# First three modulation sums on TensorE in four column groups, squares ahead of the scaling, three ScalarE products per later sum, and an output projection that is 512 columns wide

## The chip, the cores and the metric

The kernel runs on one core of one Trainium2 chip. The metric is the device time of one execution in microseconds (us). The profile is of one execution; its engines are PE (TensorE matmuls), PEld (TensorE weight loads), DVE (VectorE), ACT (ScalarE), POOL (GpSimd) and SP (the queue that issues most DMAs). "L185" is line 185 of the kernel's file; the changed kernel's lines have other numbers below the first edit.

## The reference

One transformer block on 512 tokens of width 1024, in fp32. What matters here:

```python
c_act = jax.nn.silu(c)
mod = jnp.dot(c_act, ada_w[l]) + ada_b[l]
sh1, sc1, g1, sh2, sc2, g2 = jnp.split(mod, N_MOD, axis=-1)
h = modulate(rms_norm(x, norm1_g[l]), sh1, sc1)          # h*(1+scale)+shift
z = jnp.einsum('bsd,de->bse', h, w_in[l]) + b_in[l]      # q, k, v, gates of two branches
...                                                       # mLSTM branch, attention branch
x = x + g1[:, None, :] * jnp.einsum('bsd,de->bse', merged, w_out[l])
h = modulate(rms_norm(x, norm2_g[l]), sh2, sc2)
...                                                       # gated FFN, then a last rms_norm
```

## The kernel before, in words

All matmuls with weights run as three passes of fp32r (`mm3`, L197 to L201): high part by high part, high by low, low by high. Weights come from HBM in chunks; `cvt` makes the high part (a cast on ACT, L183) and the low part (a subtraction on DVE, L185). Each engine works its own queue in the order in which the code is written; the order is set by hand, and for later stages by a planner that counts the time of each matmul (`spend`).

**The first stage (L475 to L577).** The rows of x (four tiles of 128 tokens, two halves each) are squared, normalised and scaled (`normed`, L408), two tiles at a time: sums of squares of tiles 0 and 1, their reciprocal root, their scaling, then the same for tiles 2 and 3. TensorE turns the tiles (`turn_x`), ACT keeps the turned tiles (`keep_x`). The stage then computes seven blocks of 128 output columns over eight blocks k of the width: 21 matmuls of 512 columns per k (`g1_mm`, L554, order in L567 to L577: seven with the high weights, seven with the low weights, seven with the low part of h). Each k needs its own tile of h (`h_tile`, L512: high part `hh` on ACT, low part `hl` on DVE), and that needs the modulation of block k: shift and scale, a sum over eight products of a 128x256 piece of `ada_w` with a column of silu(c), and over the 128 partitions.

For k = 0 TensorE does this whole sum with 16 fp32 matmuls (L500). For k = 1 to 7 `ada_fast` (L271) shares the products out: POOL multiplies and adds two (three for k = 1), DVE multiplies and adds four (three), ACT multiplies two, POOL adds all, and `ada_cols` (L304) sums over the partitions with two one-column matmuls against ones. `ada_put` (L298) writes shift and scale with two small DVE instructions. In each k from 2 on, at the ninth matmul, `ahead` (L532) sends out: the cast of the next weights, the sum for k+2, the modulation and h tile of k+1, the low part of the next weights.

POOL also works out the angles of the rotary embedding: half of them ahead of the stage (`next(turns)`, L477), half behind the last modulation sum (L575). ACT takes their sine and cosine (L565, L566) ahead of the results of the stage, which it moves out of PSUM (`padded`, L589). The convolutions, the gates (L849) and all later work follow from there; L754 is where TensorE turns the gates.

**The output projection (L1206 to L1324).** `project` multiplies a tile of 128 tokens of the merged branches (eight blocks of the width, stationary) by a chunk of `w_out`. A chunk holds all eight row blocks of 256 output columns, so there are four chunks, 16 calls, each with 24 matmuls of 256 columns. Each result is multiplied by the gate and added to x on DVE (L1227, L1229, 256 wide); `squares` sums the squares on ACT, `normed2` finishes the second norm for two token tiles, and `h2_part` turns and modulates the result for the FFN. The FFN begins with token tiles 0 and 1 (`first`, L1340) while tiles 2 and 3 are being finished.

Of the kernel before, what the change touches and what calls it, by code (L numbers as in the profile page):

```python
# [40 lines left out]
def _chunks():  # L41
# [18 lines left out]
    for q in range(4):  # L60
        got.append(("w_out", 0, 8, 256 * q, 256))
# [38 lines left out]
def block_kernel(ctx, tc, x, wall, adaw, pcol, prow, positions, inv_freq, out):  # L100
# [60 lines left out]
    def cvt(n, half, what=None, eng=None):  # L161
# [19 lines left out]
        s = slice(0, SIZES[n]) if half is None else slice(half * h, half * h + h)  # L181
        if what != "lo":
            A.copy(hi[:, s], raws[n][:, s])  # L183
# [87 lines left out]
    def ada_fast(j, pools, vs, scaled, between=None):  # L271
        p = small([128, 256], "accp", 3)
        for k in pools:
            t = small([128, 256], "prod", 2) if k else p
            G.tensor_scalar(t[:], araw[j][k], cact[:, k:k + 1], 1.0, op0=ALU.mult, op1=ALU.mult)
            if k:
                G.tensor_tensor(out=p[:], in0=p[:], in1=t[:], op=ALU.add)
        a = small([128, 256], "accv", 2)
        for k in vs:
            if k == vs[0]:  # L280
                V.tensor_scalar(a[:], araw[j][k], cact[:, k:k + 1], None, op0=ALU.mult)
            else:
                V.scalar_tensor_tensor(out=a[:], in0=araw[j][k], scalar=cact[:, k:k + 1], in1=a[:],
                                       op0=ALU.mult, op1=ALU.add)
            if between and k == vs[1]:
                between()
        for t in (scaled() if callable(scaled) else scaled) + [a[:]]:
            G.tensor_tensor(out=p[:], in0=p[:], in1=t, op=ALU.add)  # L288
        return p
# [14 lines left out]
    def ada_cols(b, j, acc):  # L304
        pb = bank("c")
        for q in range(2):
            PE.matmul(pb[:, q:q + 1], acc[:, blk(q)], ones[:, 0:1], start=True, stop=True)
# [45 lines left out]
    A.activation(cact[:], cols[:, 0:8], AF.Silu)  # L353
    hcol = const.tile([128, 60], F32, name="hcol")
# [44 lines left out]
    def rms_tiles(tiles):  # L399
        n = len(tiles)  # L400
        ss = small([128, 5, n], f"ss{n}", 3)
# [3 lines left out]
        rms_finish(ss, D)  # L405
        return [ss[:, 3, i:i + 1] for i in range(n)]

    def normed(tiles, between=None):  # L408
        rs = rms_tiles(tiles)
        if between:  # L410
            between()
        got = [[T(), T()] for _ in tiles]
        for q in range(2):
            for i, r in enumerate(rs):
                if i % 2 == q:
                    V.tensor_scalar(got[i][q][:], tiles[i][q][:], r, None, op0=ALU.mult)
                else:
                    A.activation(got[i][q][:], tiles[i][q][:], AF.Copy, scale=r)
        return got
# [57 lines left out]
    next(turns)  # L477

    wb = bank("c")
# [4 lines left out]
    xb = [bank(t) for t in ("m", "m", "a", "a", "a")]  # L484
    ab = [bank("b"), bank("c")]
# [5 lines left out]
    def keep_x(k):  # L491
        xnT[k] = T()
        A.copy(xnT[k][:], xb[k][:])

    for k in range(5):
        turn_x(k, (0, 1))
    xn += normed(xt[2:4])
    for k in range(KD):
        for q in range(2):
            PE.matmul(ab[q][:, :128], araw[0][k][:, blk(q)], cact[:, k:k + 1].to_broadcast([128, 128]),  # L500
                      start=k == 0, stop=k == KD - 1)
    for k in range(5):
        turn_x(k, (2, 3))
    ada_put(0, 0, ab[0][:, 0:1], ab[1][:, 0:1])
    xb += [bank(t) for t in "bbc"]
    for k in range(5, KD):
        turn_x(k, range(NT))
# [4 lines left out]
    def h_tile(k):  # L512
        src = xnT[k] if k else xb[0]
# [3 lines left out]
        V.tensor_scalar(hf[:], src[:], modA[:, k:k + 1], modB[:, k:k + 1], op0=ALU.mult, op1=ALU.add)  # L517
        V.tensor_tensor(out=pr[1][:], in0=hf[:], in1=pr[0][:].bitcast(F32), op=ALU.subtract)
        hT.append(pr)

    cvt(0, None)
    h_tile(0)
    for k in range(1, 5):
        keep_x(k)
    accs = ada_fast(1, range(3), (5, 6, 7), ada_scaled(1, (3, 4)))
    cvt(1, None)
    for k in (5, 7, 6):
        keep_x(k)
    g1 = [bank(t) for t in ("m", "m", "a", "a", "a", "b", "b")]
    for k in range(KD):  # L530
        wh, wl = parts[k]
        def ahead():  # L532
# [5 lines left out]
            def following():  # L538
                ada_cols(0, k + 1, ready)
                h_tile(k + 1)  # L540

            if k + 2 < KD:
                accs = ada_fast(k + 2, (0, 1), (2, 3, 4, 5),
                                (lambda: ada_scaled(2, (6, 7))) if k == 0 else ada_scaled(k + 2, (6, 7)),
                                None if k else following)
                if k + 4 < KD:
                    ada_fetch(k + 4)
            if 0 < k < KD - 1:
# [23 lines left out]
        for n, (m, e) in enumerate(order):  # L572
            if n == (16, 14, 8)[min(k, 2)]:
# [635 lines left out]
    def parts_of(n):  # L1209
        return tuple(t.rearrange("p (k n) -> p k n", k=8) for t in parts[n])  # L1210

    nb = [0]

    def project(ch, ci, tiles, n=0):
        pbs = []
        for _ in tiles:
            pbs.append(bank(mb[nb[0] % 4]))
            nb[0] += 1
# [318 lines left out]
```

## Time and profile before

| | us |
|---|---|
| three timed runs | 800.43, 801.29, 801.38 (median 801.29) |
| the profiled execution | 800.23, of which the span from first to last instruction is 798.4 |
| mean granted TensorE clock | 0.996 |

| engine | busy us | share of the span |
|---|---|---|
| PE | 781.0 | 98% |
| PEld | 652.7 | 82% |
| DVE | 410.1 | 51% |
| POOL | 323.5 | 41% |
| ACT | 306.8 | 38% |

The shares are means over stages that differ. From 30 to 50 us DVE and POOL are busy for more than 90% of the time, elsewhere mostly for less than 70%. A matmul's row shows when it started and a modelled end that overlaps the next one's start, so the pace of matmuls is read from the distance of their starts. A row's part in brackets is the idle time of the engine ahead of it and what ended it.

### The profile page before, as it was taken

What the parts mean: (1) busy time and instruction counts of PE and PEld (TensorE: products, weight loads), DVE (VectorE), ACT (ScalarE), POOL (GpSimd) and SP (SyncE); (2) the same over time, 40 slices, a digit from 0 to 9 for tenths busy, and PEclk for the clock granted to TensorE, in tenths of its full rate; (3) what the DMA queues carried; (4) which work ended last, traced back from release to release, by engine and by line L of the source; (5) the groups of instructions that cost most, each with busy time, mean ns of one, the idle gap of its engine ahead of it and who ended that gap; (6) DMA issues with size and microseconds to landing.
All of it is one profiled execution on the core that took longest, in us unless ns stands there. A gap on an engine that the chain in (4) does not pass through costs nothing.

```text
span 798.4 us, 10508 instructions
## 1 busy us (share of the span) xinstructions
PE 781.0 (98%) x4049; PEld 652.7 (82%) x4049; DVE 410.1 (51%) x665; ACT 306.8 (38%) x535; POOL 323.5 (41%) x446
## 2 busy tenths in 40 slices
PE   8899999999999999999999999999999999999995
PEld 8678988778877787788999988888888888888884
DVE  6986778665575553477557333222322324333257
ACT  6538654324454444323257322212222213333234
POOL 7894436899965878950002695000000000000013
PEclk9999999999999999999999999999999999999998
DMA  8936224345421432345222325532233232222002
GB/s 316 377 118 225 106 80 151 100 172 211 159 106 54 155 109 106 140 186 202 75 86 106 118 107 173 234 107 67 93 105 106 106 105 106 99 67 99 1 0 106
DMA packets 23538, 102.52 MB, mean 128 GB/s; under 512 B 3512, under 2 KB 3648, under 8 KB 13888
## 3 DMA queue, kind: packets, MB, share of 16 engines
q1 hardware_dynamic: 21664, 99.74, 34.8%
q10 hardware_dynamic: 1824, 2.12, 1.0%
q8 instruction: 32, 0.52, 0.3%
q14 instruction: 18, 0.15, 0.1%
HBM read 97.65 MB, written 2.10 MB: 125 GB/s over the span
## 4 chain that ended last, share of the span: by engine, by line
PE 83%; DVE 7%; POOL 4%; ACT 3%; issue 1%; DMA 1%; SPq 0%; POOLq 0%; DVEq 0%; ACTq 0%
PE psm L198 14%; PE psm L200 14%; PE psm L199 14%; PE psb L198 9%; PE psb L200 9%; PE psb L199 9%; PE psa L200 2%; PE psa L198 2%; PE psa L199 2%; POOL accp L288 2%; PE psa L1038 1%; PE psc L1096 1%; DVE x L1433 1%; PE psb L1079 1%; DVE t L611 1%
## 5 line engine op out<-in xcount | busy, mean ns | idle before, releaser
L185 DVE TENSOR_TENSOR whl<-raw,whl 128x1024 fp32r<-128x1024 f32 (+1 forms) x124 | 159.0, 1292 | 181.4 <-ACT whl L183 181.3
L183 ACT CAST whl<-raw 128x1024 fp32r<-128x1024 f32 (+1 forms) x124 | 127.7, 1050 | 277.3 <-PE psb L200 162.2
L1436 POOL TENSOR_TENSOR t<-x,v 128x512 f32<-128x512 f32 x6 | 7.8, 1306 | 284.1 <-DVE x L1433 279.6
L251 POOL TENSOR_TENSOR accp<-accp,prod 128x256 f32<-128x256 f32 x112 | 89.9, 803 | 9.3
L198 PE MATMUL psb<-t,whl 128*128 128x512 f32 (+1 forms) x224 | 84.4, 377 | 0.0
L198 PE MATMUL psm<-t,whl 128*128 128x512 f32 (+1 forms) x224 | 84.3, 376 | 0.0
L200 PE MATMUL psb<-t,whl 128*128 128x512 f32 (+1 forms) x224 | 84.0, 375 | 0.0
L200 PE MATMUL psm<-t,whl 128*128 128x512 f32 (+1 forms) x224 | 83.8, 374 | 0.0
L199 PE MATMUL psm<-t,whl 128*128 128x512 f32 (+1 forms) x224 | 83.8, 374 | 0.0
L199 PE MATMUL psb<-t,whl 128*128 128x512 f32 (+1 forms) x224 | 83.8, 374 | 0.0
L198 PE MATMUL psm<-hh,whl 128*128 128x512 f32 x192 | 77.4, 403 | 0.5 <-ACT x L1020 0.5
L248 POOL TENSOR_SCALAR prod<-ada,cact 128x256 f32<-128x256 f32 x112 | 75.6, 675 | 0.0
L200 PE MATMUL psm<-hh,whl 128*128 128x512 f32 x192 | 75.0, 391 | 0.0
L199 PE MATMUL psm<-hl,whl 128*128 128x512 f32 x192 | 74.9, 390 | 0.0
L200 PEld LDWEIGHTS psb<-t,whl 128*128 128x128 f32 x224 | 42.1, 188 | 7.9 <-DVE whl L185 0.2
L200 PEld LDWEIGHTS psm<-t,whl 128*128 128x128 f32 x224 | 42.2, 188 | 7.5
L199 PEld LDWEIGHTS psm<-t,whl 128*128 128x128 f32 x224 | 42.2, 188 | 7.5
L199 PEld LDWEIGHTS psb<-t,whl 128*128 128x128 f32 x224 | 42.2, 188 | 7.5
L198 PEld LDWEIGHTS psm<-t,whl 128*128 128x128 f32 x224 | 42.2, 188 | 7.4
L198 PEld LDWEIGHTS psb<-t,whl 128*128 128x128 f32 x224 | 42.2, 188 | 7.3
L198 PEld LDWEIGHTS psm<-hh,whl 128*128 128x128 f32 x192 | 36.1, 188 | 8.1 <-ACT x L1020 0.7
L200 PEld LDWEIGHTS psm<-hh,whl 128*128 128x128 f32 x192 | 36.0, 188 | 8.2 <-DVE whl L185 0.4
(371 smaller groups left out, 1635.9 us busy)
## 6 DMA issues: line engine op xcount, KB each, us to landing
raw<-in_dram SPq DMA_DIRECT2D x59, 1024.0 KB, 4.8
ada<-in_dram SPq DMA_DIRECT2D x16, 1024.0 KB, 4.8
t<-in_dram SPq DMA_DIRECT2D x30, 256.0 KB, 5.8
x<-in_dram SPq DMA_DIRECT2D x16, 256.0 KB, 5.7
raw<-in_dram SPq DMA_DIRECT2D x8, 448.0 KB, 6.1
v<-in_dram SPq DMA_DIRECT2D x8, 256.0 KB, 5.6
t<-t ACTq DMA_DIRECT2D x32, 64.0 KB, 2.1
out_dram<-t SPq DMA_DIRECT2D x8, 256.0 KB, 2.1
```

The source lines that it names most:

```text
L183: A.copy(hi[:, s], raws[n][:, s])
L185: (eng or V).tensor_tensor(out=lo[:, s], in0=raws[n][:, s], in1=hi[:, s].bitcast(F32), op=ALU.subtract)
L198: PE.matmul(o, lh, rh, start=start, stop=False)
L199: PE.matmul(o, lh, rl, start=False, stop=False)
L200: PE.matmul(o, ll, rh, start=False, stop=stop)
L248: G.tensor_scalar(t[:], rv[:, k, :], cact[:, k:k + 1], 1.0, op0=ALU.mult, op1=ALU.mult)
L251: G.tensor_tensor(out=p[:], in0=p[:], in1=t[:], op=ALU.add)
L288: G.tensor_tensor(out=p[:], in0=p[:], in1=t, op=ALU.add)
L611: V.scalar_tensor_tensor(out=y[:, e:], in0=zr[:, :512 - e], scalar=hcol[:, 32 - e * 8 + m:33 - e * 8 + m], in1=y[:, e:], op0=ALU.mult, op1 ...
L1038: PE.matmul(bs[e][:, o:o + n], qp[a][r, blk(i)], kp[b][r, :n], start=g == 0, stop=g == 2)
L1079: PE.transpose(tb[:, o + (i - j) * 128:o + (i - j + 1) * 128], es[i][:, blk(j)], ident[:])
L1096: PE.matmul(yb[e * 64:e * 64 + 64, 128 * j:512], av[j][:, (2 * p + e) * 64:(2 * p + e + 1) * 64], t[j], start=j == 0, stop=j == NT - 1)
```

## The change

Five things are changed together.

1. The modulation sums of k = 0, 1 and 2 are computed on TensorE. The stationary operand is 32 equal columns of silu(c), the moving operand the 128x256 piece of `ada_w`; products k and k+4 go to output partitions 32(k mod 4) and up, four column groups in one PSUM bank. ACT copies the bank out, and two one-column matmuls with a column that is 1 on one partition of each group add the four groups and turn the result. For k = 1 they are sent out behind the sixth matmul of k = 0, for k = 2 behind the fourth of k = 1.
2. For k = 3 to 7 ACT does three products rather than two, the first of which is the start of DVE's sum; DVE's own first product goes.
3. The sums of squares of all four x tiles are started ahead of the first scaling, POOL does three of the eight scalings, all four tiles are turned for six of eight k (the other two inside k = 0), the first 640 columns of the first weights are cast by POOL, and the first half of the angles stands behind that cast on POOL.
4. The code that emits the work ahead is placed at other matmuls for k = 0 and 1.
5. A chunk of `w_out` holds four row blocks of 512 columns. `project` then does 12 matmuls of 512 columns per call, the second chunk adds to the first one's bank, and gating, adding to x and squaring are 512 wide.

```diff
-        got.append(("w_out", 0, 8, 256 * q, 256))
+        got.append(("w_out", 512 * (q % 2), 4, 512 * (q // 2), 512))
...
+    def ada_rows(j):
+        pb = bank("c")
+        for k in range(8):
+            g = slice(k % 4 * 32, k % 4 * 32 + 32)
+            PE.matmul(pb[g, :256], cact32[:, k, :], araw[j][k], start=k < 4, stop=k >= 4)
+        t = T()
+        A.copy(t[:, 0:256], pb[:, 0:256])
+        return t
+
+    def ada_fast(j, pools, vs, scaled):
...
+        lead, *rest_ = ada_scaled(j, scaled)
         a = small([128, 256], "accv", 2)
         for k in vs:
-            if k == vs[0]:
-                V.tensor_scalar(a[:], araw[j][k], cact[:, k:k + 1], None, op0=ALU.mult)
...
+            V.scalar_tensor_tensor(out=a[:], in0=araw[j][k], scalar=cact[:, k:k + 1],
+                                   in1=lead if k == vs[0] else a[:], op0=ALU.mult, op1=ALU.add)
+        for t in rest_ + [a[:]]:
             G.tensor_tensor(out=p[:], in0=p[:], in1=t, op=ALU.add)
...
-    for _ in range(23):
+    for _ in range(30):
         PE.matmul(wb[:, :128], ident[:], ones, start=True, stop=True)
-    xn = normed(xt[0:2])
+    xn = [[T(), T()] for _ in range(NT)]
+    s01 = sums(xt[0:2])
+    rms_open(s01, D)
+    s23 = sums(xt[2:4])
+    rms_close(s01)
+    for i, q, eng in ((0, 0, V), (1, 0, A), (0, 1, G), (1, 1, G)):
+        scaled_by(eng, xn[i][q], xt[i][q], s01[:, 3, i:i + 1])
+    rms_open(s23, D)
+    rms_close(s23)
+    for i, q, eng in ((2, 0, V), (3, 0, A), (2, 1, V), (3, 1, G)):
+        scaled_by(eng, xn[i][q], xt[i][q], s23[:, 3, i - 2:i - 1])
...
+    for k in range(6):
         turn_x(k, (0, 1))
+    r0 = ada_rows(0)
+    for k in range(2):
         turn_x(k, (2, 3))
+    keep_x(0, V)
+    ada_cols(0, 0, r0, sel4[:], "b")
+    for k in range(2, 6):
+        turn_x(k, (2, 3))
...
+    cvt(0, slice(0, 640), "hi", G)
+    next(turns)
+    keep_x(1)
+    h_tile(0, lambda: cvt(0, slice(0, 640), "lo"))
...
-                accs = ada_fast(k + 2, (0, 1), (2, 3, 4, 5),
...
+            if 1 < k < KD - 2:
+                accs = ada_fast(k + 2, (0, 1), (2, 3, 4), (5, 6, 7))
...
-            if n == (16, 14, 8)[min(k, 2)]:
+            if k == 0 and n == 4:
+                for kk in (7, 6):
+                    turn_x(kk, range(NT))
+                for kk in (7, 5, 6):
+                    keep_x(kk)
+            if n == (6, 4, -1)[min(k, 2)]:
+                third = early()
+            if n == (13, 10, 8)[min(k, 2)]:
                 ahead()
...
+    def project(ch, half, i, q):
+        if half == 0:
+            pbank[i] = bank(mb[i])
+        pb = pbank[i]
+        for k in range(4):
+            m = mg[4 * half + k]
+            mm3(pb[:], m[0][:, blk(i)], m[1][:, blk(i)], ch[0][:, k, :], ch[1][:, k, :],
+                half == 0 and k == 0, half == 1 and k == 3)
+        if half:
+            tm = T()
+            V.tensor_tensor(out=tm[:], in0=pb[:], in1=g1row[q][:], op=ALU.mult)
...
     def squares(i, q):
-        h = xr[i][0][:] if q == 0 else xr[i][1][:, (q - 1) * 256:q * 256]
         junk = T()
-        A.activation(junk[:, :512 if q == 0 else 256], h, AF.Square, accum_out=sq[:, q, i:i + 1])
+        A.activation(junk[:], xr[i][q][:], AF.Square, accum_out=ss2[i // 2][:, q, i % 2:i % 2 + 1])
```

On DVE, around the first reciprocal root of the first stage (`ss` holds the sums, `x` are halves of x tiles), before the change:

```order
L392 SCALAR_TENSOR_TENSOR ss_36_240<-ss_36_240 128x1 x2
L393 SCALAR_TENSOR_TENSOR ss_36_240<-ss_36_240 128x2
L416 TENSOR_SCALAR t_256<-x_87,ss_36_240 128x512
L416 TENSOR_SCALAR t_259<-x_92,ss_36_240 128x512
L376 SCALAR_TENSOR_TENSOR t_282,ss_52_281<-x_95 128x512
L376 SCALAR_TENSOR_TENSOR t_286,ss_52_281<-x_99 128x512
```

and now:

```order
L388 SCALAR_TENSOR_TENSOR t_260,ss_48_259<-x_95 128x512
L388 SCALAR_TENSOR_TENSOR t_264,ss_48_259<-x_99 128x512
L401 RECIPROCAL ss_43_247<-ss_43_247 128x2
L404 SCALAR_TENSOR_TENSOR ss_43_247<-ss_43_247 128x1 x2
L405 SCALAR_TENSOR_TENSOR ss_43_247<-ss_43_247 128x2
L424 TENSOR_SCALAR t_239<-x_87,ss_43_247 128x512
```

The squares of tiles 2 and 3 (`x_95`, `x_99`) stood behind the scaling of tiles 0 and 1 and now stand ahead of their reciprocal.

On TensorE inside k = 0 of the first stage there is nothing but matmuls with weights (`whl`) in the kernel before. Now this stands there (`cact` is silu(c), `t_113` to `t_119` the modulation weights of k = 1, `sel` the selecting column):

```order
L578 MATMUL psm_372<-hh_358,whl_337 128x512
L276 MATMUL psc_399<-t_113,cact_169 32x256 x2
L276 MATMUL psc_399<-t_115,cact_169 32x256 x2
L276 MATMUL psc_399<-t_117,cact_169 32x256 x2
L276 MATMUL psc_399<-t_119,cact_169 32x256 x2
L578 MATMUL psm_373<-hh_358,whl_337 128x512
L578 MATMUL psa_374<-hh_358,whl_337 128x512
L578 MATMUL psa_375<-hh_358,whl_337 128x512
L578 MATMUL psa_376<-hh_358,whl_337 128x512
L578 MATMUL psm_372<-hl_359,whl_337 128x512
L578 MATMUL psm_373<-hl_359,whl_337 128x512
L578 MATMUL psa_374<-hl_359,whl_337 128x512
```

Eight matmuls of 256 columns in four groups came in between.

On DVE in a later k (here k = 4; `accv` is DVE's part of the sum for k+2), before:

```order
L281 TENSOR_SCALAR accv_602<-t_494,cact 128x256
L283 SCALAR_TENSOR_TENSOR accv_602<-t_494,cact,accv_602 128x256
L283 SCALAR_TENSOR_TENSOR accv_602<-t_496,cact,accv_602 128x256 x2
L300 SCALAR_TENSOR_TENSOR modA<-psc_618,adb_170,cols 128x1
L302 TENSOR_TENSOR modB<-psc_618,cols 128x1
L517 TENSOR_SCALAR t_623<-t_363,modA,modB 128x512
L518 TENSOR_TENSOR hl_625<-t_623,hh_624 128x512
L185 TENSOR_TENSOR whl_591<-raw_452,whl_591 128x896
```

and now:

```order
L291 SCALAR_TENSOR_TENSOR accv_607<-t_492,cact,t_601 128x256
L291 SCALAR_TENSOR_TENSOR accv_607<-t_492,cact,accv_607 128x256
L291 SCALAR_TENSOR_TENSOR accv_607<-t_494,cact,accv_607 128x256
L306 SCALAR_TENSOR_TENSOR modA<-psc_622,adb_178,cols 128x1
L308 TENSOR_TENSOR modB<-psc_622,cols 128x1
L527 TENSOR_SCALAR t_627<-t_368,modA,modB 128x512
L530 TENSOR_TENSOR hl_629<-t_627,hh_628 128x512
```

One instruction of eight went; the first that is left reads ACT's product `t_601`.

## Rows read from the trace of the kernel before

**Rows 1.** Waits of PEld over the whole run: total us, times, longest.
```profile
PEld psm L556 <- DVE whl L185: 3.6, 5, 1.0
PEld psa L754 <- DVE gates L849: 0.9, 1, 0.9
```

**Rows 2.** Chain of waits, followed back from 110 or 100 us: start, us, what.
```profile
55.17 0.80 POOL accp L288
...
62.24 0.37 ACT t L565
...
91.68 0.27 PE psa L754
```

**Rows 3.** Timeline of DVE in k = 4: start, us, engine, line, what.
```profile
45.84 0.48 DVE L281 TENSOR_SCALAR accv<-t,cact 128x256 f32<-128x256 f32 x1
...
46.36 2.33 DVE L283 SCALAR_TENSOR_TENSOR accv<-t,cact,accv 128x256 f32<-128x256 f32 x3
...
50.64 1.08 DVE L185 TENSOR_TENSOR whl<-raw,whl 128x896 fp32r<-128x896 f32 x1
...
51.64 0.48 DVE L281 TENSOR_SCALAR accv<-t,cact 128x256 f32<-128x256 f32 x1
```

**Rows 4.** Timeline of PE in the first stage.
```profile
17.76 0.48 PE L556 MATMUL psm<-hh,whl 128*128 128x512 f32 x1
...
18.62 0.50 PE L556 MATMUL psm<-hh,whl 128*128 128x512 f32 x1 [0.38 <-DVE t L517]
...
31.19 0.73 PE L556 MATMUL psm<-hh,whl 128*128 128x512 f32 x2 [0.30 <-ACT hh L516]
...
40.42 0.50 PE L307 MATMUL psc<-ones_r,accp 128*128 128x1 f32 x4
...
40.78 0.47 PE L556 MATMUL psm<-hh,whl 128*128 128x512 f32 x1
```

**Rows 5.** Timeline ahead of the first stage, all engines.
```profile
5.39 0.69 DVE L376 SCALAR_TENSOR_TENSOR t<-x 128x512 f32<-128x512 f32 x1
...
8.98 0.17 DVE L389 RECIPROCAL ss<-ss 128x2 f32<-128x2 f32 x1 [0.23 <-ACT ss L384]
...
10.05 1.21 DVE L416 TENSOR_SCALAR t<-x,ss 128x512 f32<-128x512 f32 x2
...
11.87 0.39 PE L500 MATMUL psb<-cact,v 128*128 128x128 f32 x2
...
15.44 0.60 PE L489 MATMUL psm<-ident,t 128*128 128x128 f32 x4
```

**Rows 6.** Timeline of SP: the DMA that is issued when a slot is free.
```profile
9.84 0.33 SPq L260 DMA_DIRECT2D t<-in_dram  x1
```

**Rows 7.** Groups by line and shape: busy us, mean ns of one, idle before.
```profile
L1021 POOL TENSOR_SCALAR t<-t 128x512 f32<-128x512 f32 x8 | 4.9, 618 | 0.6 <-ACT t L1020 0.6
...
L1190 DVE TENSOR_TENSOR t<-t,psb 128x512 f32<-128x512 f32 x4 | 2.7, 679 | 0.0
```

**Rows 8.** Timeline of PE: fp32 matmuls in two column groups, and what follows.
```profile
251.89 2.38 PE L1096 MATMUL psc<-t,t 128*64 128x512 f32 x16
...
254.19 0.50 PE L198 MATMUL psm<-hh,whl 128*128 128x512 f32 x1
```

**Rows 9.** Timeline of PE: 24 matmuls of 512 columns, and the whole projection.
```profile
66.22 0.39 PE L198 MATMUL psc<-hh,whl 128*128 128x512 f32 x1
...
71.43 0.39 PE L200 MATMUL psc<-hh,whl 128*128 128x512 f32 x1
...
375.33 0.28 PE L198 MATMUL psm<-whl,mh 128*128 128x256 f32 x1
...
415.64 0.60 PE L1263 MATMUL psa<-ident,t 128*128 128x128 f32 x4
```

**Rows 10.** Timeline of PE and DVE at the projection's end.
```profile
424.24 0.41 DVE L1227 TENSOR_TENSOR zb<-psb,t 128x256 f32<-128x256 f32 x1
...
432.97 1.56 PE L1263 MATMUL psa<-ident,t 128*128 128x128 f32 x12 [0.62 <-DVE t L1252]
```

More of the change, by code (lines that the diff above doesn't have):

```diff
@@ L302, in ada_put, with ada_cols @@
         V.tensor_tensor(out=modB[:, s:s + 1], in0=shift, in1=cols[:, 96 + b * 16 + j:97 + b * 16 + j], op=ALU.add)
-    def ada_cols(b, j, acc):
-        pb = bank("c")
+    def ada_cols(b, j, acc, rows=None, tag="c"):
+        pb = bank(tag)
         for q in range(2):
-            PE.matmul(pb[:, q:q + 1], acc[:, blk(q)], ones[:, 0:1], start=True, stop=True)
+            PE.matmul(pb[:, q:q + 1], acc[:, blk(q)], rows or ones[:, 0:1], start=True, stop=True)
         ada_put(b, j, pb[:, 0:1], pb[:, 1:2])
@@ L353, in block_kernel @@
     A.activation(cact[:], cols[:, 0:8], AF.Silu)
+    cact32 = const.tile([128, 8, 32], F32, name="cact32")
+    V.tensor_copy(cact32[:], cact[:].rearrange("p (k o) -> p k o", o=1).to_broadcast([128, 8, 32]))
+    sel4 = const.tile([128, 1], F32, name="sel4")
+    G.memset(sel4[:], 0.0)
+    for r in range(4):
+        G.memset(sel4[r * 32:r * 32 + 1, :], 1.0)
     hcol = const.tile([128, 60], F32, name="hcol")
@@ L404, in rms_tiles, with scaled_by @@
                 sumsq(halves[q][:], ss[:, q, i:i + 1], A if q else V)
[L405 to L419, printed above, removed]
+        return ss
+    def scaled_by(eng, o, h, r):
+        if eng is A:
+            A.activation(o[:], h[:], AF.Copy, scale=r)
+        elif eng is G:
+            G.tensor_scalar(o[:], h[:], r, 1.0, op0=ALU.mult, op1=ALU.mult)
+        else:
+            V.tensor_scalar(o[:], h[:], r, None, op0=ALU.mult)
     onehot = const.tile([36, 4, 128], F32R, name="onehot")
@@ L489, in turn_x, with keep_x, h_tile @@
             PE.transpose(xb[k][:, blk(i)], xn[i][k // 4][:, blk(k % 4)], ident[:])
-    def keep_x(k):
+    def keep_x(k, eng=A):
         xnT[k] = T()
-        A.copy(xnT[k][:], xb[k][:])
-    for k in range(5):
+        (A.copy if eng is A else V.tensor_copy)(xnT[k][:], xb[k][:])
+    for k in range(6):
         turn_x(k, (0, 1))
[L497 to L502, printed above, removed]
-        turn_x(k, (2, 3))
[L504 to L507, printed above, removed]
+    r0 = ada_rows(0)
+    for k in range(2):
+        turn_x(k, (2, 3))
+    keep_x(0, V)
+    ada_cols(0, 0, r0, sel4[:], "b")
+    for k in range(2, 6):
+        turn_x(k, (2, 3))
+    xb += [bank(t) for t in "bc"]
     hT = []
-    def h_tile(k):
-        src = xnT[k] if k else xb[0]
+    def h_tile(k, between=None):
+        src = xnT[k]
         hf = T()
@@ L1280, in block_kernel @@
     ch = begin(C_OUT)
-    project(ch, 0, (0, 1), 2)
-    mid(C_OUT)
-    project(ch, 0, (2,), 1)
-    project(ch, 0, (3,), 1)
+    for i in range(NT):
+        if i == 2:
+            mid(C_OUT)
+        project(ch, 0, i, 0)
     ch = begin(C_OUT + 1)
@@ L1288, in block_kernel @@
             mid(C_OUT + 1)
-        project(ch, 1, (i,), 1)
+        project(ch, 1, i, 0)
         if i < 3:
@@ L1297, in block_kernel @@
     load(C_GU + 2)
[L1298 to L1305 removed]
+    for i in range(2):
+        project(ch2, 0, i, 1)
+    for i in range(2):
+        project(ch3, 1, i, 1)
+        squares(i, 1)
     normed2(0)
[L1307 to L1310 removed]
+    for i in range(2, NT):
+        project(ch2, 0, i, 1)
     load(C_GU + 3)
```

104 lines of the change are left out of this document (34 added, 70 removed).

## The prediction

> **What bounds the kernel now.** The page's first part, the busy shares, says TensorE: 98% of the span. Such a share is a mean, so the windows by stage were read next: from about 100 us to 780 us TensorE never rests, and every microsecond of matmul saved there, or of start gained ahead of it, moves the end. The list of waits then shows where it rests: in the first stage for the weights' low part, and once for the gates at L754, for 0.9 us [rows 1]. The chain of waits tells why it waits at L754: back from there it runs over DVE and ACT to the sine at 62.24, to POOL's angles and POOL's modulation sums [rows 2]. So up to 92 us it isn't TensorE's own work that decides but when POOL is done with the last sum (55.17 + 0.80 = 55.97) and the angles behind it (62.24, thus 6.27 later). TensorE getting through the first stage sooner only lengthens its wait at L754, unless POOL is sooner too. POOL in turn goes at DVE's pace: from one k to the next DVE's first product moves from 45.84 to 51.64, 5.80 us, without a rest [rows 3].
>
> **The price of a sum on TensorE.** No sum in four groups is in the trace. The 16 matmuls of L500 appear as 32 records of 128 columns, 4096 columns in 15.44 - 11.87 = 3.57 us, one after another [rows 5]. L1096 has two column groups: 16 records, four widths of 512 to 128 in two groups and two records each, 5120 columns. At L500's pace they would take 4.46 us; the next matmul starts 2.30 us after the first [rows 8]. So two groups run side by side nearly without loss (1.94 times). A new sum has 16 records of 256 columns, again 4096: 3.57 us one by one, 1.8 two at a time, 0.9 four at a time. I take 0.9, since the two groups of the nearest row overlapped fully, and add 0.4 for emptying the array ahead of it and behind it: a record of 512 columns is 0.39 long at a pace of 5.21/23 = 0.2265 [rows 9], a tail of about 0.2 on each side. That makes 1.3 us; the ends for the range are 1.3 and 4.0.
>
> The Trainium skill bears on this in two places. "TensorE: Matmul & The Clock Gate", Part 3, gives 2.38 times for three column groups; carried on to four (an estimate from that page) a sum would take 1.1 rather than 0.9, 0.6 us over the three. The same part says that matmuls start and end strictly in program order; if the second record of a matmul must start ahead of the next group's first, only two groups overlap. That is a rival below.
>
> **The start.** DVE now squares half of tile 3 ahead of the first reciprocal. SP's issue at 9.84 is released by that half's landing [rows 6]; with 0.69 for the square the reciprocal comes at 10.53 instead of 8.98, so scaling starts at 11.6 instead of 10.05 [rows 5]: 1.55 lost. POOL's two scalings at 0.62 each [rows 7] go behind DVE's first (0.6, half of 1.21), since POOL stretches beside DVE elsewhere: 13.4. Four turns at 0.11, the sum at 1.3: 15.2. From there as before from the last turns (15.44) to the first weight matmul (17.76), 2.3 us [rows 4, 5]: 17.5. Before, the second matmul waited until 18.62, so the stream in effect began at 18.4. Tiles 2 and 3 come out of their own root meanwhile, off this path, and POOL's cast of 640 columns ends at about 16. Gain 0.9; bounds -1.0 (POOL and DVE block each other throughout) and 1.5.
>
> **k = 0 and k = 1.** Of matmuls with weights each k has 21 at 0.2265, 4.76 us. k = 0 adds eight turns (0.9), the sum (1.3), the selecting matmuls (L307's four records take 0.36 and slow the next, 0.45 [rows 4]) and about 0.4 of waiting, as ACT copies three banks one by one behind the first `hh`: 7.8, so k = 1 starts at 25.3. That adds 1.3 + 0.45: k = 2 at 31.8. ACT (copy of the sum, three products, cast) and DVE (three products, modulation) reach the same point at about 32.0; I take 31.9. Before: 31.19 [rows 4]. So these two k give back more than the start gained: 0.7 late.
>
> **k = 2 to 7.** DVE's stretch per k loses the product of L281, 46.36 - 45.84 = 0.52 [rows 3]: 5.28. ACT's extra product hides in ACT, which rests about 3 us per k waiting for the modulation. TensorE itself needs 4.76 + 0.45 = 5.2, so nothing takes DVE's place at once. From 31.9, with 0.9 + 1.1 (the low parts of h and of the weights, the last 1.08 in rows 3) and three stretches, DVE's first product of k = 5 comes at 31.9 + 2.0 + 15.85 = 49.8 rather than 51.64. Of the 1.85, 1.56 is three times 0.52; the rest is that k = 2 and 3 took longer than 5.8 before, when POOL's sums were late. They won't be: POOL has five sums rather than seven, and begins the first at about 23, as its angles moved behind the cast. The last sum ends 55.97 - 51.64 = 4.33 behind DVE's first product, as POOL has the same six instructions per sum: 54.1. Angles 6.27: the sine at 60.4. **First term: 1.8 us.** Bounds: -1 (k = 0 and 1 a little longer, stretch not shorter) and 3.3 (TensorE's own gain at the stage's end).
>
> **The projection.** Before: 14 of 16 calls, 336 matmuls of 256 columns, from 375.33 to 415.64: 0.1200 each, 2.88 per call [rows 9]. Now 12 of 512 at 0.2265: 2.72. That is 0.16 per call, 2.25 over 14. The other two calls stand between the pieces of the FFN's input; behind them TensorE waits 0.62 for the second norm [rows 10]. There DVE moves out two tiles at 2 x 0.68 instead of 2 x 0.42 [rows 7, 10], 0.5 more each, while ACT has two squares fewer ahead of it. I count the 0.3 of these two calls as lost in that wait. The half-chunks need no new wait: each bank is read a whole chunk ahead of its next use, DVE is half idle there, and the casts have 5.4 us in place of 5.8 for some 3.4 of work. **Second term: 2.25 us**, bounds 1.2 and 2.8.
>
> **Sum.** 1.8 + 2.25 = 4.05 off the span of 798.4, of 800.23 for the profiled execution: 796.2. The median of the timed runs is 1.06 above that execution, and I forecast a median: 797.2.
>
> **Rivals.**
> - *POOL takes DVE's place* (0.20). It is on the chain itself [rows 2], its six instructions with their waits fill nearly all of 5.80. If its period stays, the 1.56 goes: first term 0.3, time 798.7. Against it: it rests when the sum starts behind DVE's low part, 4.33 of the new 5.28.
> - *TensorE's whole gain comes through* (0.15). The early sums let POOL run ahead, the angles are never late: 3.3 + 2.25, time 795.7.
> - *Two groups at a time* (0.08). A sum is 0.9 dearer, three lie on the path to k = 2: 2.7 off the first term, time 799.9. With two groups in L1096 the trace can't tell this from full overlap.
> - *The start fails* (0.06). DVE and POOL stretch each other in scaling and cast, ACT's queue of copies and casts in k = 0 holds the next modulation: k = 2 two to three us later still, time 800 to 802.
> - *Slower: the groups run one by one* (0.06). Each sum 3.57 + 0.4, 2.7 more, three of them 8.1: the stage ends 6.3 late, minus 2.25 is 4.0 slower: 805.3. It decides from 2.65 us per sum on. Against it: rows 8.
> - That the change doesn't do what it says: the projection's 512 columns stand in the instructions, so at least that term must show, except where a wait eats it; within the cases above.
>
> **How the numbers follow.** The forecast has 0.45, with a range of its own from 795.8 to 798.6. With the rivals, 8 in 10 lie from 793.2 to 801.2: on top the failed start and half of the slower case are left out, below a stage that shrinks by more than 5. What differs by less than 0.2% (1.6 us) can't be told from no change. Faster: 0.45 + 0.20 + 0.15 and a little of the others, 0.81; same: most of two at a time and of the failed start, 0.12; slower 0.07.
>
> **What would show it.** Right: L276's records start within some ns of each other across four groups, a sum lasts about 1 us; the first weight matmul near 17.5, k = 2 near 31.9; k = 3 to 6 each 5.3 apart; the sine near 60.4 and a longer wait at L754; 192 matmuls of the projection at 0.2265; TensorE's wait behind it near 1 us. Wrong: k still 5.8 apart (POOL), L276 records 0.2 apart in turn (no overlap), or new waits inside the projection.

## The result and the profile after

The changed kernel was timed six times: 795.17 to 796.31 us, median 795.64, against 799.96 to 801.38, median 800.34, for six runs of the kernel before. The ratio is 0.994 (95% interval 0.9929 to 0.9951): 4.7 us faster. Its profiled execution took 796.31 us, the slowest of the six, with a span of 794.5; before, 800.23 and 798.4. So the two traces explain 3.9 of the 4.7. The other 0.8 is the place of the two executions among their own runs: the one after is 0.67 above its median, the one before 0.11 below.

TensorE in the changed kernel, at the places that the forecast named (start, duration, operation):

```profile
17.53 0.71 PE L578 MATMUL psm<-hh,whl 128*128 128x512 f32 x2 [0.38 <-ACT hh L526]
...
20.17 1.07 PE L276 MATMUL psc<-t,cact 128*32 128x256 f32 x16
21.17 0.50 PE L578 MATMUL psm<-hh,whl 128*128 128x512 f32 x1
...
31.70 0.72 PE L578 MATMUL psm<-hh,whl 128*128 128x512 f32 x2
...
37.48 0.62 PE L578 MATMUL psm<-hh,whl 128*128 128x512 f32 x2
...
42.78 0.61 PE L578 MATMUL psm<-hh,whl 128*128 128x512 f32 x2
...
48.46 0.62 PE L578 MATMUL psm<-hh,whl 128*128 128x512 f32 x2
...
54.16 0.61 PE L578 MATMUL psm<-hh,whl 128*128 128x512 f32 x2
...
59.82 0.90 PE L578 MATMUL psm<-hh,whl 128*128 128x512 f32 x2
...
90.29 0.27 PE L783 MATMUL psa<-ident,gates 128*4 128x128 f32 x1 [0.57 <-DVE gates L878]
```

With the times of before in brackets: the first weight matmul comes at 17.53 (17.76), k = 2 at 31.70 (31.19) [rows 4], the gates are turned at 90.29 (91.68) [rows 2]. From k = 2 on a block takes 5.78, 5.30, 5.68, 5.70 and 5.66, not the 5.3 of the forecast. TensorE is not what paces it, and neither is DVE alone. This is POOL in the same stretch, which stands on the chain of waits from 30.73 to 60.86:

```profile
30.73 0.75 POOL L294 TENSOR_TENSOR accp<-accp,accv 128x256 f32<-128x256 f32 x1 [0.43 <-DVE accv L291]
...
42.62 1.07 POOL L294 TENSOR_TENSOR accp<-accp,accv 128x256 f32<-128x256 f32 x1
43.67 1.31 POOL L285 TENSOR_SCALAR accp<-t,cact 128x256 f32<-128x256 f32 x1
44.96 0.64 POOL L285 TENSOR_SCALAR prod<-t,cact 128x256 f32<-128x256 f32 x1
45.68 0.79 POOL L287 TENSOR_TENSOR accp<-accp,prod 128x256 f32<-128x256 f32 x1
46.55 1.68 POOL L294 TENSOR_TENSOR accp<-accp,t 128x256 f32<-128x256 f32 x2
48.31 1.07 POOL L294 TENSOR_TENSOR accp<-accp,accv 128x256 f32<-128x256 f32 x1
...
54.01 1.07 POOL L294 TENSOR_TENSOR accp<-accp,accv 128x256 f32<-128x256 f32 x1
```

No row behind the first has a wait in brackets: POOL works through. Its last two periods are 5.69 and 5.70, the four from 30.73 to 54.01 on average 5.82. The last sum's last addition starts at 54.01 (55.17 before, rows 2), and ACT takes the sine at 60.89 (62.24), as this row of ACT says:

```profile
60.89 0.63 ACT L587 ACTIVATE t<-ang 128x512 f32<-128x512 f32 x1 [1.50 <-POOL ang L478]
```

The projection, from its first matmul to the FFN's first one, and the wait behind it:

```profile
374.07 0.39 PE L198 MATMUL psm<-whl,mh 128*128 128x512 f32 x1
...
419.42 0.28 PE L198 MATMUL psm<-t,whl 128*128 128x256 f32 x1
...
429.18 1.56 PE L1283 MATMUL psa<-ident,t 128*128 128x128 f32 x12 [0.35 <-DVE t L1272]
```

TensorE's wait for the gates is as long as before [rows 1], in the list of waits:

```profile
PEld psa L783 <- DVE gates L878: 0.9, 1, 0.9
```

The gates are 1.39 earlier than before, the second norm's turning (429.18 for 432.97, rows 10) 3.79 earlier, so the stretch between gives 2.40. The span's 3.9 is the sum of these to 0.1.

### The profile page after: what moved, and what is told of

It is laid out like the page before. It is cut to its first block, busy times and chain, and to the rows that moved or that the text cites. A ratio compares the mean times of both kernels' runs of the same rounds, so it can differ in the third digit from the quotient of the medians.

```text
span 794.5 us, 10133 instructions
## 1 busy us (share of the span) xinstructions
PE 779.9 (98%) x3891; PEld 642.8 (81%) x3891; DVE 399.0 (50%) x635; ACT 306.1 (39%) x529; POOL 316.5 (40%) x441
## 4 chain that ended last, share of the span: by engine, by line
PE 85%; DVE 6%; POOL 4%; ACT 3%; issue 1%; DMA 1%; SPq 0%; POOLq 0%; ACTq 0%; DVEq 0%
PE psm L198 14%; PE psm L200 14%; PE psm L199 14%; PE psb L198 9%; PE psb L200 9%; PE psb L199 9%; PE psa L200 2%; PE psa L199 2%; PE psa L198 2%; POOL accp L294 1%; PE psa L1067 1%; PE psc L1125 1%; DVE x L1448 1%; PE psb L1108 1%; DVE t L640 1%
## 5 line engine op out<-in xcount | busy, mean ns | idle before, releaser
L185 DVE TENSOR_TENSOR whl<-raw,whl 128x1024 fp32r<-128x1024 f32 (+3 forms) x125 | 158.7, 1280 | 192.0 <-ACT whl L183 191.9
L183 ACT CAST whl<-raw 128x1024 fp32r<-128x1024 f32 (+2 forms) x124 | 127.2, 1046 | 278.9 <-PE psb L200 162.1
L248 POOL TENSOR_SCALAR prod<-ada,cact 128x256 f32<-128x256 f32 x112 | 73.6, 657 | 0.0
```

The source lines that it names most:

```text
L183: (eng.tensor_copy if eng else A.copy)(hi[:, s], raws[n][:, s])
L185: (eng or V).tensor_tensor(out=lo[:, s], in0=raws[n][:, s], in1=hi[:, s].bitcast(F32), op=ALU.subtract)
L248: G.tensor_scalar(t[:], rv[:, k, :], cact[:, k:k + 1], 1.0, op0=ALU.mult, op1=ALU.mult)
```

## Experiments

Each kernel was compared with the kernel before on the same chip. Starts differ from run to run with the landing of x, so stages are also told from the first weight matmul. The interval of a ratio is about 1 us wide each way or a little less, so differences of a few tenths between the variants are told by their traces and not by their times.

**Projection alone.** The kernel before with part 5 only:

```diff
-        got.append(("w_out", 0, 8, 256 * q, 256))
+        got.append(("w_out", 512 * (q % 2), 4, 512 * (q // 2), 512))
... project, squares and normed2 as in the change
```

> The kernel before with part 5 alone (the 512-wide projection). Theory A, the two terms are independent and the projection is worth what the two profiles show between its start and the second norm's turning (375.33 to 432.97 before, 374.07 to 429.18 after, 2.53 us): 2.5 us faster than before, about 797.8, and the sine still at 62.2. Rival, my forecast's term with 0.3 of it lost in the wait for the second norm: 2.25 us faster, and a wait there of about 0.9 instead of 0.62. Rival B, the first stage's earlier end moved the loads of the projection's chunks and so made part of its gain: under 2 us faster.

Measured: 798.37 (11 runs), before 800.11 (15 runs), ratio 0.9979 (0.997 to 0.9988): 1.7 us faster. In its trace:

```profile
92.52 0.27 PE L754 MATMUL psa<-ident,gates 128*4 128x128 f32 x1 [0.58 <-DVE gates L849]
...
431.34 0.91 PE L1254 MATMUL psa<-ident,t 128*128 128x128 f32 x6 [0.34 <-DVE t L1243]
```

From gates to turning 338.82 us, before 341.29 (432.97 - 91.68): 2.47 less, and the wait is 0.34, not 0.9. But the gates come 0.84 later than before; the first weight matmul comes at 18.47 instead of 17.76 in unchanged code, since the last half of x landed at 11.23 rather than 10.51 (SP's next issue, which waits for it). So the projection's own worth is theory A's, the time is not.

**First stage alone.** The changed kernel with the old projection (the diff above, reversed).

> The changed kernel with the projection of the kernel before (256 wide), so parts 1 to 4 alone. The projection alone was timed 1.74 us faster than before (0.96 to 2.4), while its trace shows 2.47 us less between the gates (92.52) and the second norm's turning (431.34) and a first stage that started 0.7 later, behind x rows that landed later. If that late start was chance: the projection is worth 2.4 to 2.5 here too, and this kernel is 2.2 to 2.3 us faster than before, about 798.0; the stretch from gates to the second norm's turning is 341.3 as before. If a 512-wide chunk costs something at the start of the program that the trace doesn't name: this kernel keeps the whole 4.7 less only 1.7, that is 3.0 us faster, about 797.2.

Measured: 798.03 (before 800.20), ratio 0.9973 (0.9962 to 0.9984): 2.2 us faster. Gates at 89.57 and turning at 430.90, thus 341.33 as before, with the old wait of 0.62. With the changed kernel's 4.7 this leaves 2.5 for the projection. The late start of the run before is then most likely chance, but this isn't shown: the two times alone add up to 3.9, the two changes together gave 4.7, and the 0.8 lies within the intervals. What parts 1, 3 and 4 are worth one by one was not run.

**Two ScalarE products per later sum, as before.**

```diff
-                accs = ada_fast(k + 2, (0, 1), (2, 3, 4), (5, 6, 7))
+                accs = ada_fast(k + 2, (0, 1), (2, 3, 4, 5), (6, 7))
... and DVE's first product is a tensor_scalar of its own again
```

> The changed kernel with two ScalarE products per later sum and four on VectorE, as before, the rest of the change kept. Theory POOL (POOL's six instructions per sum set the period of k = 3 to 7, it never rests from 30.73 to 60.86): VectorE's extra 0.49 is paid by stretching POOL a little; period 5.70 to 5.80 instead of 5.69, sine at 60.9 to 61.4, time 0 to 0.5 us above the changed kernel. Theory DVE (its stretch sets the period, as my forecast had it): 0.5 more in each of four to five k, period 6.2, sine near 63, time 2 us above the changed kernel.

Measured: 794.96 (before 800.11), ratio 0.9937 (0.9925 to 0.9949): 5.2 us faster, not slower than the changed kernel. Two of POOL's last additions, and the first:

```profile
29.22 0.83 POOL L297 TENSOR_TENSOR accp<-accp,accv 128x256 f32<-128x256 f32 x1
...
46.74 0.80 POOL L297 TENSOR_TENSOR accp<-accp,accv 128x256 f32<-128x256 f32 x1
...
52.53 0.80 POOL L297 TENSOR_TENSOR accp<-accp,accv 128x256 f32<-128x256 f32 x1
```

The period is 5.8 as before, and the four from 29.22 to 52.53 take 23.31 us; in the changed kernel they take 23.28 (30.73 to 54.01). The third product thus bought nothing over these four, as theory POOL has it, and it cost something at the beginning: the first of these additions comes 12.4 us behind the first weight matmul (16.86), in the changed kernel 13.2. There DVE's first product of k = 3 waits 2.48 us for a product of ACT, which stands behind ACT's copy of TensorE's sum. Part 2 of the change, and with it my main reason for the first term, was worth nothing.

**One of POOL's products to ScalarE.**

```diff
-                accs = ada_fast(k + 2, (0, 1), (2, 3, 4), (5, 6, 7))
+                accs = ada_fast(k + 2, (0,), (2, 3, 4), (1, 5, 6, 7))
... the same for k = 3
```

> The changed kernel with one of POOL's two products per later sum (k = 3 to 7) given to ScalarE, which then does four. Theory POOL: POOL's period loses 0.64 to 1.3 and falls below DVE's and TensorE's 5.2 to 5.3; four periods shrink by 0.4 each, sine at 59.0 to 59.5, time 1 to 1.6 us below the changed kernel, that is about 794.3. Theory DVE: its 5.69 stay, sine at 60.5 to 60.9, time within 0.3 us of the changed kernel.

Measured: 794.82 (before 800.11), ratio 0.9937 (0.9924 to 0.9949): 0.6 us more gained than by the changed kernel, half of what was expected. POOL's last additions are 5.31, 5.59, 5.32 and 5.55 apart, so the period did fall below 5.69; but the first comes 13.8 behind the first weight matmul, 0.6 later than in the changed kernel, since POOL now waits for three products of ACT.

**ScalarE's products for k = 3 ahead of its copy.**

```diff
+            made = ada_scaled(3, (5, 6, 7)) if k else None
             accs = ada_rows(k + 1)
... ada_fast takes `made` in place of products of its own
```

> The changed kernel with ScalarE's three products for the sum of k = 3 issued ahead of its copy of TensorE's sum of k = 2 (in the changed kernel ScalarE stands idle from 24.97 to 27.37 before that copy, and POOL waits 1.82 us for the products behind it). Theory POOL: POOL's add starts near 26.9 instead of 28.70 and its run of sums ends 1.8 to 2.2 us sooner if its period stays 5.69, or less if TensorE's 5.2 per k takes over; sine at 58.7 to 59.8, time 1 to 2 us below the changed kernel, about 794.2. Theory DVE: DVE's stretch starts with the modulation of k = 2 at 30.5, which this doesn't move, so the sine stays at 60.9 and the time within 0.3 us.

Measured: 795.06 (before 800.11), ratio 0.9939 (0.9925 to 0.9953): 5.05 us gained, 0.35 more than by the changed kernel where 1 to 2 were expected. The first addition came 2.05 sooner (11.15 behind the first weight matmul), as expected, and 1.3 of it were lost at once. POOL:

```profile
28.38 0.72 POOL L294 TENSOR_TENSOR accp<-accp,accv 128x256 f32<-128x256 f32 x1 [0.43 <-DVE accv L291]
...
33.55 1.61 POOL L294 TENSOR_TENSOR accp<-accp,t 128x256 f32<-128x256 f32 x2 [2.13 <-ACT t L267]
```

In the next sum POOL waits 2.13 for ACT's products, because ACT's cast of the next weights stands ahead of them and waits for TensorE itself:

```profile
31.65 0.95 ACT L183 CAST whl<-raw 128x896 fp32r<-128x896 f32 x1 [1.55 <-PE psb L579]
32.50 1.30 ACT L267 ACTIVATE t<-t,cact 128x256 f32<-128x256 f32 x3
```

The sine came 42.85 behind the first weight matmul, 0.5 sooner than in the changed kernel. After each of these edits a wait for another engine soon takes back a part of the gain.

**Both edits together, and ScalarE's products ahead of the cast in every k.**

```diff
+            made = ada_scaled(k + 2, (1, 5, 6, 7)) if 1 < k < KD - 2 else None
             if k:
                 cvt(k + 1, None, "hi")
... the last kernel only; both have the edits of the two experiments above
```

> The last two edits together: one of POOL's two products to ScalarE for k = 3 to 7, and ScalarE's products for k = 3 ahead of its copy of TensorE's sum of k = 2. If POOL alone was the bound, the late sum of k = 3 (its last add ended 13.8 us behind the first weight matmul with the fourth product alone, 12.4 with the earlier products alone) is early again and the period is 5.3 to 5.4: the sine comes 41.8 to 42.2 us behind the first weight matmul (43.4 in the changed kernel, 42.6 and 42.9 with the single edits), time 0.3 to 0.8 us below the single edits. If the period of act_four, alternating 5.3 and 5.6, is made by ScalarE's products that come behind the cast of the next weights (POOL and DVE both wait for them there), the early first sum is lost again: sine at 42.5, time as the single edits within 0.2.

> As the run before it, and ScalarE issues its four products for the sum of k + 2 ahead of the cast of the next weights in every later k (the cast waits for TensorE's release of the weights' slot, the products wait for nothing). If ScalarE's order makes the alternating 5.3 and 5.6: neither POOL nor DVE waits for a product, period 5.15 to 5.3 (TensorE's own 21 matmuls and sum columns take 5.12), sine 41.0 to 41.7 us behind the first weight matmul, time about 1 us below the single edits, 794 or less. If not: the cast comes up to 0.5 later, the low part of the weights with it, and TensorE waits more: time as the single edits or above.

Measured: 794.11 and 793.88 (before 800.23), ratios 0.9924 (0.9911 to 0.9938) and 0.9921 (0.9907 to 0.9934): 6.1 and 6.35 us faster than before, the best of all runs and 1.4 to 1.6 more than the change gained (the slowest of these nine runs took 794.63, the fastest of the changed kernel 795.17). The two can't be told apart. In both, the sine comes 42.18 behind the first weight matmul. For the first that is as expected, but what happens is a mixture of its two theories: POOL waits 3.06 for ACT's products in the sum of k = 4, so that the early first sum is lost (last additions 7.00 apart), and then the period alternates (5.30, 5.60, 5.32). For the second 41.0 to 41.7 were expected. There DVE waits for no product, POOL waits 0.5 for ACT's and 0.4 for DVE's sum in each k, and yet the period is 5.69 again. DVE there, and POOL's additions of ACT's products:

```profile
42.19 1.08 DVE L185 TENSOR_TENSOR whl<-raw,whl 128x896 fp32r<-128x896 f32 x1
43.19 0.95 DVE L291 SCALAR_TENSOR_TENSOR accv<-t,cact,t 128x256 f32<-128x256 f32 x1
44.17 1.72 DVE L291 SCALAR_TENSOR_TENSOR accv<-t,cact,accv 128x256 f32<-128x256 f32 x2
...
46.13 0.94 DVE L527 TENSOR_SCALAR t<-t,modA,modB 128x512 f32<-128x512 f32 x1
...
47.87 1.08 DVE L185 TENSOR_TENSOR whl<-raw,whl 128x896 fp32r<-128x896 f32 x1
...
42.20 3.41 POOL L294 TENSOR_TENSOR accp<-accp,t 128x256 f32<-128x256 f32 x3 [0.48 <-ACT t L267]
```

DVE never rests (47.87 - 42.19 = 5.68), though POOL does, and now it is DVE's instructions that are long: 0.95 for the first product, 0.94 for L527. POOL's three additions are long too, 3.41 beside 2.5 in the first of the two kernels. POOL has less to do, and DVE is stretched all the same. That asks for a run without POOL.

**Without POOL's part.**

```diff
-        for t in rest_ + [a[:]]:
-            G.tensor_tensor(out=p[:], in0=p[:], in1=t, op=ALU.add)
-        return p
+        return a
... and POOL's own products left out; ScalarE still makes its three
```

> The changed kernel where the modulation sums of k = 3 to 7 leave out POOL's two products and the two of ScalarE's that POOL adds; POOL does nothing for them, the other engines work as before. Theory PORT (DVE and POOL stretch each other, so that what one of them is spared the other takes; neither engine's own work is the bound): DVE's first product back to 0.48, the modulated tile (L527) to 0.55, the weights' low part to 1.0, DVE's period then 4.4 of its own and TensorE's 5.12 the bound; k = 3 to 7 5.1 to 5.2 apart, the stage's end 44.6 to 45.2 us behind the first weight matmul (47.35 in the changed kernel), time 1.8 to 2.6 us below the changed kernel. Theory DVE (its instructions are as long by themselves): L185 1.08 to 1.62 and 5.3 to 5.7 stay, time within 0.5 us of the best variant (794).

The time, 804.14, tells nothing here: one of the scalings ahead of the stage waited 10.0 us for a DMA, so the stage began at 26.86; why the slot was late was not looked into. From the first weight matmul on, DVE's groups (count, busy time, mean ns, idle before), first of the changed kernel from 37 to 60 us, then of this one from 42 to 65 us, where L285, L519 and L522 are what L291, L527 and L530 are there:

```profile
L185 DVE TENSOR_TENSOR whl<-raw,whl 128x896 fp32r<-128x896 f32 x5 | 7.1, 1424 | 0.0
L530 DVE TENSOR_TENSOR hl<-t,hh 128x512 fp32r<-128x512 f32 x5 | 4.7, 946 | 1.1 <-ACT hh L526 1.1
L291 DVE SCALAR_TENSOR_TENSOR accv<-t,cact,accv 128x256 f32<-128x256 f32 x6 | 4.2, 698 | 0.2
L527 DVE TENSOR_SCALAR t<-t,modA,modB 128x512 f32<-128x512 f32 x4 | 2.5, 626 | 0.1
L291 DVE SCALAR_TENSOR_TENSOR accv<-t,cact,t 128x256 f32<-128x256 f32 x3 | 1.9, 626 | 0.2 <-issue 0.2
```

```profile
L185 DVE TENSOR_TENSOR whl<-raw,whl 128x896 fp32r<-128x896 f32 x5 | 5.4, 1085 | 0.0
L285 DVE SCALAR_TENSOR_TENSOR accv<-t,cact,accv 128x256 f32<-128x256 f32 x8 | 3.9, 485 | 0.3
L522 DVE TENSOR_TENSOR hl<-t,hh 128x512 fp32r<-128x512 f32 x5 | 3.5, 692 | 1.5 <-ACT hh L518 1.5
L519 DVE TENSOR_SCALAR t<-t,modA,modB 128x512 f32<-128x512 f32 x4 | 2.2, 546 | 0.1
L285 DVE SCALAR_TENSOR_TENSOR accv<-t,cact,t 128x256 f32<-128x256 f32 x4 | 1.9, 484 | 3.6 <-ACT t L267 3.6
```

Beside POOL the same work takes 1424 ns instead of 1085, 946 instead of 692, 698 instead of 485: 1.2 us more per k (0.34 + 0.25 + 2 x 0.21 + 0.08 + 0.14). It isn't the DMA traffic, which is heavier in the first stretch (DMA share 0.68 against 0.51): from 35 to 42 us, with a share of 0.77, L285, L519 and L522 take 0.48, 0.55 and 0.69 here too. Alone, DVE rests 1.2 per k (0.9 ahead of its first product, 0.3 ahead of `hl`), and the matmuls against ones that sum over the partitions, one group per k, come 5.21 apart throughout (17.90, 23.11, 28.33, 33.54 and 38.75 us behind the first weight matmul), at TensorE's own pace:

```profile
44.76 0.50 PE L305 MATMUL psc<-ones_r,accv 128*128 128x1 f32 x4
...
49.97 0.50 PE L305 MATMUL psc<-ones_r,accv 128*128 128x1 f32 x4
```

That is theory PORT, with the other direction, POOL stretched by DVE, seen in the traces only: there is no run without DVE. The weights' low part is 1.08 even alone, where 1.0 was expected; the stage's end came 46.97 behind the first weight matmul, not 44.6 to 45.2, but k = 0 ran at a granted clock of 0.68, and the first selecting matmul inside the stage came at 7.27 instead of 5.36: without these 1.9 it is 45.1.

**The old order of scaling and squares at the start.**

```diff
-    s23 = sums(xt[2:4])
     rms_close(s01)
... scaling of tiles 0 and 1
+    s23 = sums(xt[2:4])
     rms_open(s23, D)
```

> The changed kernel with the start in the order of the kernel before: reciprocal and scaling of tiles 0 and 1 ahead of the squares of tiles 2 and 3. By my forecast's start (the squares of tile 3 cost the scaling of tiles 0 and 1 1.55 us, and that is the path): TensorE's first sum would start 1.5 sooner and the first weight matmul about 1 us sooner, 5.5 us behind the landing of the last x half instead of 6.5. Rival, tiles 2 and 3 are the path (their root ends 2.8 us behind the landing, their scaling, turning, copy and h follow): their squares now stand behind the scaling on DVE and ScalarE, root 0.4 to 0.7 later, first weight matmul 6.9 to 7.2 us behind the landing, time 0.2 to 0.7 us above the changed kernel.

Measured: 796.32 (before 800.23), ratio 0.9951 (0.9937 to 0.9964), about 0.8 us less gained than by the changed kernel; the intervals overlap. SP's next issue waits for the last half of x, so it shows the landing. The landing and the first weight matmul, of the changed kernel with the fourth product and of this one, and here the first turning too:

```profile
10.31 0.33 SPq L260 DMA_DIRECT2D t<-in_dram  x1
...
16.79 0.70 PE L578 MATMUL psm<-hh,whl 128*128 128x512 f32 x2 [0.38 <-ACT hh L526]
```

```profile
10.18 0.33 SPq L260 DMA_DIRECT2D t<-in_dram  x1
...
11.43 0.60 PE L502 MATMUL psm<-ident,t 128*128 128x128 f32 x4
...
16.40 0.70 PE L578 MATMUL psm<-hh,whl 128*128 128x512 f32 x2 [0.38 <-ACT hh L526]
```

The old order starts the weights 6.22 us behind the landing rather than 6.48 (6.45 to 6.71 in the seven kernels with the new one): 0.2 to 0.5 sooner, not the 1 that was expected. One reason is in the rows: DVE scales half of tile 0 from 9.15 to 9.64, but the turning at 11.43 has no wait in brackets, because TensorE is busy with its 30 matmuls against ones (L485) until then. So this run doesn't tell what the squares ahead of the scaling cost by themselves; a run with fewer of these matmuls was not made. But then TensorE waits longer for the weights' low part in k = 2:

```profile
PEld psm L578 <- DVE whl L185: 3.7, 6, 1.6
```

The longest wait is 1.6 (0.6 in the changed kernel), as DVE is late there: its L527 takes 0.94 in both kernels, but L185, beside POOL, 1.62 instead of 1.08. The sine comes 44.08 behind the first weight matmul, 0.7 later than in the changed kernel. Neither of the two theories had this. With the faster sums:

> The faster mixture (one POOL product to ScalarE, the products of k = 3 ahead of the copy) with the start in the old order, scaling of tiles 0 and 1 ahead of the squares of tiles 2 and 3. With the changed kernel's sums that order started the weights 0.5 sooner behind the landing of x, but TensorE then waited 1.6 us in k = 2 for a low part of the weights that DVE made late while POOL was busy. If that wait was a collision of DVE and POOL in this one phase, it can be gone with POOL's lighter sum, and the 0.5 stays: time 793.4 to 793.8. If the old order always costs it: a wait of 1 us or more for L185 in k = 2 again, time 794.5 to 795.2.

Measured: 794.26 (before 800.20), ratio 0.9925 (0.9912 to 0.9937). The sine comes 42.17 behind the first weight matmul, as in the new order, and the longest wait for L185 is 0.5, so the 1.6 is gone; the time can't be told from that of the new order. But x landed at 10.22 in this run (SP's issue), and the first weight matmul, at 16.71, came 6.49 behind, as in the new order. What the old order gained in the run above didn't stay.

**Column groups.** TensorE's sums in one group, and in two.

```diff
-            g = slice(k % 4 * 32, k % 4 * 32 + 32)
+            g = slice(k % 1 * 32, k % 1 * 32 + 32)
... start, stop, copy and selecting column to fit; for two groups k % 2
```

> The changed kernel with TensorE's three sums in one column group: the same eight matmuls each, all adding up in output partitions 0 to 31. If the four groups run side by side, this costs what L500 cost for as many columns, 3.5 us per sum instead of 1.0; 2.5 more for each of three sums, of which the first hides partly behind the scaling of tiles 2 and 3: first stage 5 to 7 us later, time 800 to 802.5. If the small output width or something else makes the sum cheap and not the groups: still 1.0 to 1.3 per sum, time as the changed kernel.

> The changed kernel with TensorE's three sums in two column groups (partitions 0 to 31 and 32 to 63). One group took 3.64 us per sum, four take 1.07 with the modelled end, 1.0 to the next matmul's start. If a sum's price is its columns divided by the groups, and a tail of 0.1: 1.85 to 2.0 per sum, time 0.8 x 3 = 2.4 above the changed kernel, 797.5 to 798.5. If groups start in turn and only two ever overlap (a rival of the forecast), two groups would cost as much as four: 1.0 to 1.1, time as the changed kernel.

Measured: 803.49 and 798.34 (one run each; before 800.23 and 800.20), the first above its 800 to 802.5, the second as expected. One sum and what follows it, first in one group, then in two:

```profile
22.16 3.64 PE L276 MATMUL psc<-t,cact 128*32 128x256 f32 x16
25.73 0.50 PE L578 MATMUL psm<-hh,whl 128*128 128x512 f32 x1
```

```profile
20.35 1.92 PE L276 MATMUL psc<-t,cact 128*32 128x256 f32 x16
22.20 0.50 PE L578 MATMUL psm<-hh,whl 128*128 128x512 f32 x1
```

To the next matmul's start a sum takes 3.57, 1.85 and, with four groups, 1.00: the columns divided by the groups, and about 0.1. It is the groups that make the sum cheap, and without them the change was 3 us slower than before in the one run: the forecast's slower rival was nearly of the right size (805.3), and false.

## Why the prediction was right, point by point

The predicted time was 797.2 (range 793.2 to 801.2), 4.1 below the median shown; measured 795.64, 4.7 below the median of the runs of before beside it.

- **The price of a sum** (1.3, bounds 1.3 and 4.0): 1.00, below the lower bound. The 0.9 for full overlap was right; of the 0.4 for emptying the array, 0.1 is there. The Trainium skill, "TensorE: Matmul & The Clock Gate", Part 3, gives 2.38 for three groups; here two give 3.57 / 1.85 = 1.93 and four 3.57, by the starts. The case that only two groups overlap is out.
- **The start** (first weight matmul at 17.5): 17.53 in the profiled execution, but x landed late there (10.81; 10.51 in the profile of before). In the seven kernels with this sum and this order of the start it is 16.44 to 17.53, mostly near 16.8. Behind the landing it is 6.71 here and 6.45 to 6.48 in the other six, where the old start has 7.25 and 7.24 (before, projection alone). With the stream in effect from 18.4 on before, as the forecast counts, the gain is 1.2 to 1.4 rather than 0.9. The late start is also the likeliest place of the 0.67 by which the profiled execution is above its median; the first weight matmul of the timed runs was not seen.
- **k = 0 and k = 1** (k = 2 at 31.9): 31.70.
- **k = 2 to 7: the step that failed.** "DVE's stretch per k loses the product of L281 ... 5.28" and "nothing takes DVE's place at once". The blocks took 5.62 on average (59.82 - 31.70 over five). POOL, "against it: it rests" in my rival, didn't rest once. Its six instructions are long because DVE's are, and the other way round: what one engine was spared, the other took, and taking L281 away brought nothing (23.28 for four sums, 23.31 with the product back on DVE). The rival that POOL takes DVE's place [rows 2] had the mechanism; its time, 798.7, was too high, since POOL's start of the sum for k = 3 (last addition at 30.73, before 32.73) gave 2.0 us, of which 0.8 went in the four sums behind it (23.28 for 22.44). So the last sum ended at 55.08 and not at 54.1; that the sine came only 0.5 late (60.89 for 60.4) is luck, as the angles took 5.81 instead of 6.27.
- **The first term** (1.8): 1.35 at the sine, 1.39 at the gates. The wait for the gates stayed at 0.9 [rows 1], it didn't grow as forecast: the stage's end came 1.34 sooner (64.88 for 66.22), the sine 1.35.
- **The projection** (2.25): 2.40 to 2.47 from gates to turning. The 0.3 that I gave away to the wait for the second norm was not lost. That wait is 0.35, where 0.62 stood before; it didn't grow to 1. The stretch from the projection's first matmul (375.33, rows 9) to the FFN's (423.14) was 47.81, now it is 45.35 (374.07 to 419.42).
- The forecast's sum of the two terms, 4.05, stands beside 3.9 in the traces: 0.4 too much for the first, 0.15 to 0.2 too little for the second. The total came out well because these two errors are small and opposite.

The Trainium skill has the rule that I had not weighed: "SBUF — State Buffer", the section "Who interferes with whom", says that a DVE instruction with two SBUF inputs contends with a GpSimd instruction that reads SBUF. The runs agree for L185, L530 and L291 (two tile inputs each, 1.29 to 1.44 times as long beside POOL). L527 has one tile input and is 1.15 times as long on average; why it is longer too was not tested.

## What to carry to other kernels

When two engines that slow each other are both busy for over 90% of a stage, taking an instruction off one gives little: read what the other does in that moment, and move work to an engine outside the pair (here TensorE for whole sums, ScalarE for POOL's products, TensorE's two one-column matmuls instead of more additions). Before counting a saving per turn of a loop, look for the second engine that has no waits in its rows. And a product handed to an idle engine is only cheap if it doesn't stand behind a waiting instruction in that engine's queue.

## What the runs showed of the hardware that wasn't expected

- DVE and POOL: the same DVE instructions take 1.15 to 1.44 times as long beside POOL (the two groups of rows above); in the changed kernel POOL's L285 of 128x256 takes 0.48 at 24.69, where DVE rests for the larger part of it, and 1.83 at 37.39 beside DVE's low parts of h and of the weights.
- Four column groups of 32 overlap almost fully in fp32: 1.00 us for what takes 3.57 in one group.
- The same start came up to 1.1 us apart (16.44 to 17.53 in seven kernels), mostly by the landing of x (9.97 to 10.81); differences of a microsecond between two profiled executions are to be read from a common point.
- Where the stage began late (the kernel without POOL's part), TensorE rested 8.4 us, the granted clock was 0.73 from 18 to 25 us and 0.68 from 25 to 35 us (means, partly at 1.2 GHz, partly at 2.4), and its first pair of 512-column matmuls took 1.19 where 0.71 stands else; from 35 us on the clock was 1.00 (2.4 GHz).
